# New issue orders for VectorE and ScalarE at the entries of a Strassen-Winograd convolution and of two feed-forward blocks

## The chip, the cores and the metric

The kernel runs on 1 core of one Trainium2 chip. The metric is device microseconds of one execution. Five engines work side by side, each through its own instructions in order: TensorE (PE, matmul; its weight loads are PEld), VectorE (DVE), ScalarE (ACT), GpSimd (POOL) and SyncE (SP); ACT, POOL and SP also issue DMA transfers. Engines wait for one another through semaphores only.

## The reference

A decoder trunk on x of 1024 tokens by 1024 features, all in fp32, two layers deep. With h = rms_norm(x, g) = x * rsqrt(mean(x*x) + 1e-6) * g:

```python
# layer 0                                   # layer 1
b, c, u = split(h @ w_in, 3)                q, k, v = h @ w_qkv        # 16 heads of 64
y = causal_depthwise_conv(c * u, 3 taps)    o = three dilated windows, merged by softmax of their lse
x = x + (b * y) @ w_out                     x = x + o @ w_out
# after each layer, a feed-forward block
x = x + (silu(h @ w_gate) * (h @ w_up)) @ w_down      # 1024 -> 2816 -> 1024
# at the end: rms_norm(x, final gain)
```

## The kernel before, in words

**Number format.** Every fp32 operand of a matmul is split into a high and a low part in a reduced format: ScalarE copies the high part (`split`, L139; `hi`, L567), VectorE subtracts it from the source for the low part (L140, L568). A product of blocks is three matmuls: high times high, high times low, low times high (L575, L576, L577 in `mm`). So twelve matmuls make one 128 x 512 output over a depth of 512: four operand tiles k = 0 to 3, three matmuls each; the low part of operand tile k is first read by the second of its three, the low part of the weight by the third matmul of the product.

**Winograd's form.** The convolution's input projection and both feed-forward blocks multiply 2 x 2 blocks with seven products instead of eight. The seven are numbered m = 1, 2, 6, 5, 7, 3, 4. The activations give seven operands (`b[m]`, four tiles each); the weights of one unit u (two output tiles of 128) give seven weight blocks, some of them sums of raw weight blocks made on VectorE (`combo`, L191). One product is (u, m). A unit's results gather in three PSUM banks: p takes m = 1, 6, 7, 4; q takes m = 2; r takes m = 5, 3. On the way ScalarE copies p out after m = 1, 6 and 7 (`save`, L581; tiles u1, u2, u3, each half a page of SBUF), and VectorE adds banks to them (`add`, L585): u1 + q is the output quarter (0, 0), made by `first`; u3 + r is quarter (1, 1), after m = 5 and 7; u2 + r is quarter (0, 1), after m = 3; p after m = 4 is quarter (1, 0). PSUM has eight banks, and a product that starts a bank waits until the earlier owner of that bank has been read; a product that adds to r waits until VectorE has read r.

**Orders.** `unit_order` writes the sequence of products by hand. At the start, unit by unit results are interleaved, since operands m = 6, 7, 5, 4, 3 are only made while m = 1 and 2 run. The product with index n in that order:
- convolution: (0,1) (1,1) (0,2) (1,2) (2,1) (2,2) (3,1) (3,2) (4,1) (4,2) (0,6) (1,6) (0,7) (1,7) (0,5) (1,5) (0,4) (1,4) (0,3) (1,3) (2,6) (2,5) (2,7) (3,6) ...
- first feed-forward block (key 0): (0,1) (1,1) (0,2) (1,2) (2,1) (2,2) (3,1) (3,2) (0,6) (1,6) (0,7) (1,7) (0,4) (1,4) (0,5) (1,5) (0,3) (1,3) (2,6) (2,5) (2,7) (3,6) ...
- second feed-forward block (key 1): (0,1) (1,1) (2,1) (3,1) (0,2) (1,2) (2,2) (3,2) (4,1) (4,2) (0,6) (1,6) (0,7) (1,7) (0,4) (1,4) (0,5) (1,5) (0,3) (1,3) (2,6) (2,5) (2,7) (3,6) ...

There is no planner: every engine's instructions are in the order in which the program issues them. After each product `products` calls `filled(n)`, and that calls `start(n)`, where the entry's further work is placed by n: next steps of the generator that makes operands (`operands` in the convolution, `second_half` in the feed-forward blocks), squares and sums for the norm, and `ensure(i)`, which issues weight sums and splits up to place i in the list of weights. `mm` itself calls `ensure` for `self.ahead` products ahead. `ensure` also makes SyncE fetch raw weight rows (512 KB each) into pages; a fetch waits for a free page. `at(u, m)` is the place of a weight in the list.

**The norm.** `stats` has two steps. The first sums the accumulated squares on TensorE (L485), takes the root on ScalarE (L488), the reciprocal (L489) and a diagonal matrix (L494) on VectorE; the second spreads the result over partitions by a matmul (L501) that ScalarE copies out (`rstd`, L502). Square root and Silu stand in different activation tables of ScalarE, so a root after other work begins with a table load; a dummy activation on a `scratch` column can make that load early. `flush` issues a sum of squares that was put off.

**The feed-forward entries.** The operands are made from scaled columns. `first_half` makes operands 1 and 2 from the left half of the columns while the layer before still writes the right half. `gained` scales the right half by the gain, and POOL adds two of these tiles by an accumulating DMA (L1183; `xd`). `second_half` scales them by `rstd` (L1187) and makes operands 7, 6, 4, 5, 3 in that order. `out` applies Silu to a gate quarter (L1239, ScalarE, even units) and multiplies the matching up quarter by it (L1242, VectorE, odd units); `store` sends quarters to DRAM on POOL's queue.

**Pages.** SBUF tiles of 128 x 1024 share 41 pages, half tiles 20 half pages; in the second block's entry x, operands, weight splits and raw rows fill the pages.

Of the kernel before, what the change touches and what calls it, by code (L numbers as in the profile page):

```python
# [95 lines left out]
def trunk(ctx: ExitStack, tc: tile.TileContext, x, gains_in, cwi, ck, cwo, wqkv, wo, relb,  # L96
# [444 lines left out]
    class Strassen:  # L541
# [75 lines left out]
        def whole(self, u, m, d):  # L617

            if m == 1:
                d["p"] = self.bank()  # L620
            elif m in (2, 5):
                d["q" if m == 2 else "r"] = self.bank()
            self.mm((u,), m, d["q" if m == 2 else "r" if m in (5, 3) else "p"], m in (1, 2, 5))
            if m in (1, 6, 7):
                d[{1: "u1", 6: "u2", 7: "u3"}[m]] = self.save(d["p"])
            if (u, m) == (0, 6):
                self.first(0)
            if m == 4:
                self.out(u, (1, 0), d.pop("p"))
            elif m == 3:  # L630
                self.out(u, (0, 1), self.add(d.pop("u2"), d.pop("r")))
            elif m in (5, 7) and "u3" in d and "r" in d:
                self.out(u, (1, 1), self.add(d.pop("u3"), d["r"]))
            early = self.key != 0
            if m == 2 and u > 3 + early or (u, m) in ((1, 3) if self.key == 1 else (0, 4), (3, 7)):
                for x in {u * (u < 2): range(4), 3: (4,) * early}.get(u, (u,)):
                    self.out(x, (0, 0), self.first(x))
                    del self.st[x]["u1"]

# [263 lines left out]
    class Conv(Strassen):  # L903
# [167 lines left out]
        def mix(self, group1):  # L1071
# [3 lines left out]
            def start(n):  # L1075
# [38 lines left out]
                elif n == 14:  # L1114
                    ensure(self.at(0, 3))
                    next(prep, None)
                    later = sums_of.pop(("m", (CONV, 2), 6))
                    ensure(self.at(1, 3))
                    later()
                    X[:] = [None] * KT  # L1120
                elif n == 18:
                    self.ahead = 3
                elif n == 19:
                    self.first(4)
                if 8 < n < 13:
                    self.squares((n - 5,), 1)
                if n == 16:
                    norm.joined()

            def gather():  # L1130
# [15 lines left out]
    class Swiglu(Strassen):  # L1146
# [27 lines left out]
        def gained(self, n):  # L1174
# [6 lines left out]
            if n > 3:  # L1181
                self.xd[n - 4] = self.xg[n - 4]
                nc.gpsimd.dma_start(out=self.xd[n - 4], in_=t, accum_op=ALU.add)  # L1183

        def second_half(self):

# [8 lines left out]
            if self.key:  # L1195
                yield
                self.first(0)
                self.first(1)
            for k in range(4):
# [14 lines left out]
            lows = [self.hi(4, k, f[4 + k]) for k in range(4)]  # L1214
            if self.key:
                for lo in lows:
                    lo()
                lows = []
            for k in range(4):
# [27 lines left out]
        def feed_forward(self, stats, last_step, after, final=None):  # L1247
            prep = []

            def start(n):  # L1250
# [6 lines left out]
                if n == 1 + self.key:  # L1257
                    next(stats)
                if n == 1:
                    if self.key:  # L1260
                        for m in (6, 7):
                            combos[self.key, 1](m)
                    ensure(self.at(0, 6))
                if n == 2 + 2 * self.key:
                    run(stats)
                    prep.append(self.second_half())
                    next(prep[0])
                    nc.scalar.activation(scratch, eps, AF.Silu)
                if n == 2:
                    ensure(self.at(1, 6))  # L1270
                elif n == 4:
                    ensure(self.at(1, 7))
                if n in ((5, 7, 8, 9, 11), (5, 6, 11, 12, 13, 16))[self.key]:
                    ensure(self.base + n + 3)
                    next(prep[0], None)

            self.run(start)
# [29 lines left out]
    def into_ffn(i, norm):  # L1307
# [50 lines left out]

        def last_step():
            run(pre[0])  # L1360
            norm.flush()

# [631 lines left out]
```

## Time and profile before

| | us |
|---|---|
| median of 3 runs (2137.76 to 2138.27) | 2137.87 |
| the profiled execution | 2138.59 |
| its span in the profile | 2136.8 |
| TensorE busy, share of the span | 2117.3, 99% |
| VectorE busy | 1718.8, 80% |
| ScalarE busy | 992.4, 46% |
| granted TensorE clock, mean | 0.998 |

The profiled execution's own time is 1.8 us more than its span. In the span, the convolution's first product starts at 5.5 us, the first feed-forward block's at 331.0 and the second one's at 1484.7; attention lies between. A line of a timeline reads: start, length, engine, line, operation, output<-inputs, shapes, count, and in brackets the idle time of the engine before it and what ended that. A line of the windows reads: stretch, then busy time and instruction count of PE, PEld, DVE, ACT and POOL, then the granted clock, the DMA share and GB/s.

### The profile page before, as it was taken

The numbers are of one execution on the slowest core, as the hardware profiler recorded it, in microseconds if no ns is written. First come the engines' busy times: TensorE is split into PE (matmuls) and PEld (weight loads), VectorE is DVE, ScalarE is ACT, GpSimd is POOL, SyncE is SP. The second block draws the span as 40 slices with busy tenths as digits, with TensorE's granted clock in tenths as the row PEclk, the third lists the DMA queues.
The fourth block names the chain that finished last, engine by engine and source line by source line (L and its number), as shares of the span: only waits on it lengthen the run. The fifth ranks groups of instructions, "written<-read, shape, count | busy, mean of one in ns | idle before, by whom it ended". The sixth has DMA issues, their size and how long they took to land.

```text
span 2136.8 us, 30748 instructions
## 1 busy us (share of the span) xinstructions
PE 2117.3 (99%) x11086; PEld 1815.5 (85%) x11086; DVE 1718.8 (80%) x3160; ACT 992.4 (46%) x1782; POOL 221.9 (10%) x316
## 2 busy tenths in 40 slices
PE   9999999999999999999999999999999999999998
PEld 7788888888888888878999999888788888888887
DVE  8898769888888888864676767768888888878876
ACT  7433336444544443344545454536544544444435
POOL 2000001111212000010111111110011212100000
PEclk9999999999999999999999999999999999999999
DMA  7222643334545784342333333635125545586432
GB/s 214 69 94 69 237 143 88 124 123 161 180 153 170 262 305 152 108 135 65 88 102 97 103 98 95 205 123 188 33 81 174 168 153 180 172 338 199 156 94 80
DMA packets 149347, 308.82 MB, mean 145 GB/s; under 512 B 50106, under 2 KB 61386, under 8 KB 149194
## 3 DMA queue, kind: packets, MB, share of 16 engines
q1 hardware_dynamic: 83306, 208.92, 30.6%
q0 software_dynamic: 25872, 79.02, 10.5%
q10 hardware_dynamic: 40016, 18.90, 3.0%
q8 instruction: 88, 1.44, 0.3%
q14 instruction: 65, 0.53, 0.1%
HBM read 209.06 MB, written 88.28 MB: 139 GB/s over the span
## 4 chain that ended last, share of the span: by engine, by line
PE 77%; issue 10%; DVE 7%; DMA 3%; ACT 2%; POOL 0%; SPq 0%; DVEq 0%; ACTq 0%; POOLq 0%
PE bank L575 16%; PE bank L577 16%; PE bank L576 16%; PE bank L1584 4%; PE bank L371 4%; PE bank L369 4%; PE bank L370 4%; PE bank L670 2%; PE bank L673 2%; PE bank L672 2%; PE bank L1444 1%; PE bank L1443 1%; PE bank L1442 1%; PE bank L1509 1%; PE bank L1508 1%
## 5 line engine op out<-in xcount | busy, mean ns | idle before, releaser
L575 PE MATMUL bank<-b,w 128*128 128x512 f32 x1816 | 710.0, 391 | 3.8 <-ACT w L139 2.2
L577 PE MATMUL bank<-b,w 128*128 128x512 f32 x1816 | 707.0, 389 | 2.1 <-DVE w L140 2.1
L576 PE MATMUL bank<-b,w 128*128 128x512 f32 x1816 | 707.7, 390 | 0.6 <-DVE b L568 0.3
L575 PEld LDWEIGHTS bank<-b,w 128*128 128x128 f32 x1816 | 341.1, 188 | 77.4 <-ACT w L139 5.2
L577 PEld LDWEIGHTS bank<-b,w 128*128 128x128 f32 x1816 | 341.0, 188 | 74.6 <-DVE w L140 3.4
L576 PEld LDWEIGHTS bank<-b,w 128*128 128x128 f32 x1816 | 341.2, 188 | 71.2 <-DVE b L916 1.1
L139 ACT ACTIVATE w<-combo 128x512 fp32r<-128x512 f32 (+2 forms) x448 | 229.3, 540 | 249.6 <-DVE combo L191 229.7
L140 DVE TENSOR_TENSOR w<-combo,w 128x512 fp32r<-128x512 f32 (+2 forms) x448 | 254.7, 581 | 30.8 <-ACT w L139 30.5
L581 ACT ACTIVATE part<-bank 128x512 f32<-128x512 f32 x168 | 100.2, 597 | 295.9 <-PE bank L577 292.2
L140 DVE TENSOR_TENSOR w<-raw,w 128x512 fp32r<-128x512 f32 (+2 forms) x308 | 169.4, 568 | 23.3 <-ACT w L139 23.1
L585 DVE TENSOR_TENSOR part<-part,bank 128x256 f32<-128x256 f32 (+1 forms) x328 | 154.2, 500 | 35.4 <-ACT part L581 20.0
L139 ACT ACTIVATE w<-raw 128x512 fp32r<-128x512 f32 (+2 forms) x308 | 150.9, 527 | 63.8 <-DMA raw<-in_ffn_w_down 19.1
L831 DVE TENSOR_TENSOR x<-x,bank 128x512 f32<-128x512 f32 x168 | 114.7, 683 | 37.2 <-PE bank L577 34.6
L369 PE MATMUL bank<-w_hi,w 128*128 128x512 f32 (+1 forms) x320 | 119.6, 374 | 0.0
L371 PE MATMUL bank<-w_hi,w 128*128 128x512 f32 (+1 forms) x320 | 117.8, 368 | 0.3 <-DVE w L140 0.3
L370 PE MATMUL bank<-w_lo,w 128*128 128x512 f32 (+1 forms) x320 | 117.7, 368 | 0.0
L506 DVE TENSOR_TENSOR x<-x,bank 128x512 f32<-128x512 f32 (+1 forms) x104 | 66.0, 642 | 56.0 <-PE bank L371 47.0
L369 PE MATMUL bank<-h_hi,w_hi 128*128 128x512 f32 x256 | 104.4, 408 | 0.0
L191 DVE TENSOR_TENSOR combo<-raw 128x512 f32<-128x512 f32 (+1 forms) x160 | 103.2, 645 | 0.0
L371 PE MATMUL bank<-h_hi,w_lo 128*128 128x512 f32 x256 | 100.0, 391 | 0.2 <-DVE w_lo L140 0.2
L370 PE MATMUL bank<-h_lo,w_hi 128*128 128x512 f32 x256 | 99.9, 390 | 0.0
L1603 ACT ACTIVATE z<-bank 64x512 f32<-64x512 f32 x32 | 19.0, 594 | 160.6 <-PE bank L1584 160.4
(266 smaller groups left out, 3816.7 us busy)
## 6 DMA issues: line engine op xcount, KB each, us to landing
hin<-part SPq DMA_DIRECT2D x126, 256.0 KB
raw<-in_ffn_w_gate SPq DMA_DIRECT2D x44, 512.0 KB
raw<-in_ffn_w_up SPq DMA_DIRECT2D x44, 512.0 KB
b<-ready SPq DMA_DIRECT2D x42, 512.0 KB
part<-sum POOLq DMA_DIRECT2D x72, 256.0 KB, 3.5
raw<-in_ffn_w_down SPq DMA_DIRECT2D x48, 384.0 KB
x<-spill SPq DMA_DIRECT2D x24, 512.0 KB
raw<-in_attn_w_qkv SPq DMA_DIRECT2D x24, 512.0 KB
```

What stands on the lines that cost most here:

```text
L139: nc.scalar.activation(hi, src, AF.Copy)
L140: eng.tensor_tensor(out=lo, in0=src, in1=hi, op=ALU.subtract)
L191: eng.tensor_tensor(out=c, in0=a, in1=b, op=op)
L369: nc.tensor.matmul(b, whi[:, a], ahi[:, s], start=first, stop=False)
L370: nc.tensor.matmul(b, whi[:, a], alo[:, s], start=False, stop=False)
L371: nc.tensor.matmul(b, wlo[:, a], ahi[:, s], start=False, stop=last)
L575: nc.tensor.matmul(b, hi[:, a], bhi, start=start and k == 0, stop=False, skip_group_check=True)
L576: nc.tensor.matmul(b, hi[:, a], blo, start=False, stop=False, skip_group_check=True)
L577: nc.tensor.matmul(b, lo[:, a], bhi, start=False, stop=k == n - 1, skip_group_check=True)
L581: nc.scalar.activation(t, b, AF.Copy)
L585: nc.vector.tensor_tensor(out=t, in0=t, in1=b, op=ALU.add)
L831: nc.vector.tensor_tensor(out=X[n][:, half(h)], in0=X[n][:, half(h)], in1=b, op=ALU.add)
```

## The change

Five groups of edits; no arithmetic is added or taken away, except one dummy root on one column.

- Quarters: in the feed-forward blocks quarter (0, 0) of units 0 to 3 was put out together, after (0,4) in the first block and after (1,3) in the second. Now units 0 and 1 are put out after (0,4), units 2 and 3 after (2,5), in both. The convolution's order of quarters stays.
- Convolution: clearing X, the weight split of (1,3) and the weight sums of unit 2 go from n = 14 to n = 15; the join of the two sums of squares from n = 16 to n = 18, followed by a dummy root; splits run three products ahead from n = 20 instead of 18.
- Second block, start: the copies of p after m = 1 of units 0 to 2, the weight sums of unit 1 and the splits (now up to (4,2)) are issued at n = 2, behind the root and its diagonal; the spread of `rstd` and the first part of `second_half` at n = 3 instead of 4. The splits of m = 6 follow at n = 5, those of m = 7 at n = 6.
- Second block, operands: `second_later` takes the rest in other portions, at n = 4, 5, 6, 7, 11, 13, 15, 16.
- Both blocks: `last_step` flushes the last sum of squares ahead of the last low part of operand 2.

```diff
@@ Strassen.whole
-            if m in (1, 6, 7):
+            if m in (6, 7) or m == 1 and not (self.key == 1 and u < 3):
                 d[{1: "u1", 6: "u2", 7: "u3"}[m]] = self.save(d["p"])
...
             early = self.key != 0
-            if m == 2 and u > 3 + early or (u, m) in ((1, 3) if self.key == 1 else (0, 4), (3, 7)):
-                for x in {u * (u < 2): range(4), 3: (4,) * early}.get(u, (u,)):
-                    self.out(x, (0, 0), self.first(x))
-                    del self.st[x]["u1"]
+            done = {(0, 4): range(4), (3, 7): (4,) * early}
+            if self.key != CONV:
+                done.update({(0, 4): (0, 1), (2, 5): (2, 3)})
+            for x in (u,) if m == 2 and u > 3 + early else done.get((u, m), ()):
+                self.out(x, (0, 0), self.first(x))
+                del self.st[x]["u1"]
@@ Conv.mix, start
                 elif n == 14:
                     ensure(self.at(0, 3))
                     next(prep, None)
+                elif n == 15:
                     later = sums_of.pop(("m", (CONV, 2), 6))
                     ensure(self.at(1, 3))
                     later()
                     X[:] = [None] * KT
-                elif n == 18:
+                elif n == 20:
                     self.ahead = 3
...
-                if n == 16:
+                if n == 18:
                     norm.joined()
+                    nc.scalar.activation(scratch, eps, AF.Sqrt)
@@ Swiglu, new
+        def second_later(self, low7, t3, t2, h, f, rstd, tt):
+
+            def operand(m, x):
+                for lo in [self.hi(m, k, x[k]) for k in range(4)]:
+                    lo()
+
+            self.first(0)
+            for k in range(4):
+                tt(t2[k], t3[k], f[k], ALU.add)
+            yield
+            self.first(1)
+            for lo in low7:
+                lo()
+            yield
+            operand(6, t2)
+            for k in range(4):
+                tt(f[4 + k], f[4 + k], t2[k], ALU.subtract)
+            for k in range(4):
+                tt(h[k], h[k], rstd, ALU.mult)
+            yield
+            for k in range(4):
+                tt(f[k], h[k], t2[k], ALU.subtract)
+            yield
+            operand(4, {k: f[4 + k] for k in range(4)})
+            yield
+            operand(5, f)
+            yield
+            lows = [self.hi(3, k, h[k]) for k in range(4)]
+            for lo in lows[:2]:
+                lo()
+            yield
+            for lo in lows[2:]:
+                lo()
+            X[:] = [None] * KT
@@ Swiglu.second_half
             if self.key:
                 yield
-                self.first(0)
-                self.first(1)
+                yield from self.second_later(low7, t3, t2, h, f, rstd, tt)
+                return
...
             lows = [self.hi(4, k, f[4 + k]) for k in range(4)]
-            if self.key:
-                for lo in lows:
-                    lo()
-                lows = []
@@ Swiglu.feed_forward, start
                 if n == 1 + self.key:
                     next(stats)
-                if n == 1:
+                if n == 1 + self.key:
                     if self.key:
+                        for u in range(3):
+                            self.st[u]["u1"] = self.save(self.st[u]["p"])
                         for m in (6, 7):
                             combos[self.key, 1](m)
-                    ensure(self.at(0, 6))
-                if n == 2 + 2 * self.key:
+                        ensure(self.at(4, 2))
+                    else:
+                        ensure(self.at(0, 6))
+                if n == 2 + self.key:
                     run(stats)
                     prep.append(self.second_half())
                     next(prep[0])
                     nc.scalar.activation(scratch, eps, AF.Silu)
-                if n == 2:
+                if n == 2 and not self.key:
                     ensure(self.at(1, 6))
-                elif n == 4:
+                elif n == 4 and not self.key:
                     ensure(self.at(1, 7))
-                if n in ((5, 7, 8, 9, 11), (5, 6, 11, 12, 13, 16))[self.key]:
+                if n in ((5, 7, 8, 9, 11), (4, 5, 6, 7, 11, 13, 15, 16))[self.key]:
                     ensure(self.base + n + 3)
                     next(prep[0], None)
+                if self.key and n in (5, 6):
+                    ensure(self.at(1, n + 1))
@@ into_ffn, last_step
+            norm.flush()
             run(pre[0])
-            norm.flush()
```

## The prediction

> **What bounds the kernel now.** I read the page's part 1, then the TensorE waits, then the TensorE timeline around each wait, then VectorE's and ScalarE's timelines there.
>
> ```profile
> PE 2117.3 (99%) x11086; PEld 1815.5 (85%) x11086; DVE 1718.8 (80%) x3160; ACT 992.4 (46%) x1782; POOL 221.9 (10%) x316
> ...
> 60.00:65.00 5.00, 3.44 (x16) 2.81 (x16) 4.96 (x9) 1.62 (x3) 0.00 (x0) 1.00 0.30 100
> ...
> 1595.00:1600.00 5.00, 5.00 (x24) 4.14 (x23) 2.93 (x6) 2.63 (x5) 0.00 (x0) 1.00 0.01 2
> ```
>
> TensorE sets the end; whatever is to be won is the time in which its next matmul starts late. A matmul's row lasts 0.39 but the next starts 0.23 later, and a product of twelve takes 2.72:
>
> ```profile
> 1506.76 0.39 PE L575 MATMUL bank<-b,w 128*128 128x512 f32 x1
> ...
> 1509.48 0.40 PE L575 MATMUL bank<-b,w 128*128 128x512 f32 x1
> ```
>
> So lateness is read from starts. Here are the late starts at the three entries, each with its predecessor where one is needed (convolution; first FFN; second FFN):
>
> ```profile
> 59.70 0.39 PE L577 MATMUL bank<-b,w 128*128 128x512 f32 x1
> 61.65 0.47 PE L575 MATMUL bank<-b,w 128*128 128x512 f32 x1 [1.56 <-ACT w L139]
> ...
> 336.26 0.39 PE L577 MATMUL bank<-b,w 128*128 128x512 f32 x1
> 337.09 1.05 PE L485 MATMUL bank<-ones,acc 128*128 128x1 f32 x8 [0.44 <-DVE acc L470]
> ...
> 374.65 0.40 PE L576 MATMUL bank<-b,w 128*128 128x512 f32 x1
> 375.73 0.50 PE L577 MATMUL bank<-b,w 128*128 128x512 f32 x1 [0.68 <-DVE w L140]
> ...
> 1499.08 0.39 PE L577 MATMUL bank<-b,w 128*128 128x512 f32 x1
> 1500.31 1.12 PE L501 MATMUL bank<-diag,ones 128*128 128x512 f32 x2 [0.84 <-DVE diag L494]
> 1501.51 0.40 PE L576 MATMUL bank<-b,w 128*128 128x512 f32 x1
> ...
> 1531.03 0.39 PE L577 MATMUL bank<-b,w 128*128 128x512 f32 x1
> 1531.58 0.50 PE L575 MATMUL bank<-b,w 128*128 128x512 f32 x1 [0.15 <-ACT gate L1239]
> ...
> 1535.28 0.47 PE L575 MATMUL bank<-b,w 128*128 128x512 f32 x1 [0.69 <-DVE gate L1242]
> ...
> 1538.69 0.49 PE L575 MATMUL bank<-b,w 128*128 128x512 f32 x1 [0.41 <-ACT b L567]
> 1539.51 0.50 PE L576 MATMUL bank<-b,w 128*128 128x512 f32 x1 [0.33 <-DVE b L568]
> ...
> 1550.55 0.39 PE L576 MATMUL bank<-b,w 128*128 128x512 f32 x1
> 1552.20 0.50 PE L577 MATMUL bank<-b,w 128*128 128x512 f32 x1 [1.27 <-DVE w L140]
> ```
>
> Convolution: 61.65-59.70-0.23 = 1.72. First FFN: 337.09-336.26-0.23 = 0.60 and 375.73-374.65-0.23 = 0.85, together 1.45. Second FFN: 1500.31-1499.08-0.23 = 1.00; 1531.58-1531.03-0.23 = 0.32; then, by whole products, 1535.28-1531.58-2.72 = 0.98 and 1538.69-1535.28-2.72 = 0.69; 1539.51-1538.69-0.23 = 0.59; 1552.20-1550.55-0.23 = 1.42; together 5.00. The sum is 8.17 us: nearly all that this change can win.
>
> A rule bears on how to count this. The idle times in the brackets add to 6.37 us only. The Trainium skill (Perfetto Trace Analysis, Identifying the Most-Contended Engine) calls matmul busy time a bad measure, because matmuls are pipelined, and sends the reader to weight-load time. The row of 60 to 65 agrees: weight loads fall from 4.14 to 2.81, which is 1.6 us of a slice, nearer to 1.72 than to the 1.56 idle. By idle time the forecast below would be 1.8 us later; I go by the starts.
>
> **Convolution.** The profile names ScalarE's split as what ended the 1.56, but that split is the weight of (2,6), one product later. Product (1,3), which starts at 61.65, adds into the bank that VectorE reads for (1,5):
>
> ```profile
> 58.90 0.68 DVE L140 TENSOR_TENSOR w<-combo,w 128x512 fp32r<-128x512 f32 x1
> ...
> 60.82 0.68 DVE L585 TENSOR_TENSOR part<-part,bank 128x512 f32<-128x512 f32 x1
> 61.42 1.22 DVE L449 TENSOR_TENSOR acc<-acc,acc 128x1024 f32<-128x1024 f32 x1
> ...
> 61.00 1.15 ACT L139 ACTIVATE w<-combo 128x512 fp32r<-128x512 f32 x2 [3.37 <-DVE combo L191]
> ```
>
> The read ends at 61.50; the product starts 0.15 later. The change issues the weight low (58.90), the two combinations between, and the clearing of X one product later, so the read takes the place of the low at 58.90 and ends at 59.58 (VectorE runs without a pause here). (1,3) can start at 59.93 (59.70+0.23): 1.72 gone. What is late next: the low of (1,3) now ends at 60.18, needed 0.45 into the product (60.38); the combinations end at 61.51, ScalarE's high of (2,6) at 62.2, its low at 62.9; (2,6) starts at 62.65 and needs the low at 63.10. Both margins are about 0.2, so up to 0.3 may come back. The join of the squares (1.22) moves behind that low and ends near 64.7; the sums read it after (2,6), at 65.4. The weight splits made two instead of three products ahead for two products, and the rows that SyncE fetches for them, come 2.72 later but are first needed at (2,5) and (2,7), 2 us after they are made. The early root adds one instruction to ScalarE; its table load moves. Prices from the second FFN's pair of the same kind:
>
> ```profile
> 1505.27 1.28 ACT L1268 ACT_TABLE_LOAD   x1
> 1506.57 0.20 ACT L1268 ACTIVATE scratch<-eps 128x1 f32<-128x1 f32 x1
> ```
>
> 1.5 us on ScalarE after 62.2 lie in its idle time (3.37 before 61.00); the next high, of (2,5), is then ready at 64.4 for a product at 67. Convolution: -1.7 (0 to +0.3 back).
>
> **First FFN.** The flush ahead of the last low swaps two VectorE rows:
>
> ```profile
> 335.74 0.69 DVE L568 TENSOR_TENSOR b<-hcol,b 128x512 fp32r<-128x512 f32 x1 [0.16 <-ACT b L567]
> 336.35 0.69 DVE L470 TENSOR_TENSOR acc<-acc,sq 128x512 f32<-128x512 f32 x1
> ...
> 372.40 1.28 DVE L585 TENSOR_TENSOR part<-part,bank 128x512 f32<-128x512 f32 x2
> 373.78 0.69 DVE L1242 TENSOR_TENSOR part<-part 128x512 f32<-128x512 f32 x1
> ...
> 374.99 0.68 DVE L140 TENSOR_TENSOR w<-combo,w 128x512 fp32r<-128x512 f32 x1
> ```
>
> The add then ends at 336.18, before the product ahead ends (336.49): 0.60 gone. The low ends at 336.8, for a product that starts at 337.4. Quarters: units 2 and 3 leave (0,4) for (2,5), so the 2 adds, 1 multiply, 1 Silu and 1 store on POOL's queue are issued seven products later. The low of (1,5) at 374.99 moves ahead by 3 x 0.6 = 1.8, more than the 0.85 it is late. Two banks and two half pages are held longer; with p0, p1, q0 and q1 free by then, the next banks find room. What bounds this unseen hold: 0, or a bank wait as in the rows of 1531.58 and 1535.28 (0.32 to 0.98); I take 0, because four banks are free. First FFN: -1.45.
>
> In the second FFN the flush changes nothing (its add is issued earlier already).
>
> **Second FFN.** VectorE's 128x512 rows start 0.60 apart (four in 2.50), ScalarE's 0.52 (four in 2.19):
>
> ```profile
> 1494.30 1.06 ACT L581 ACTIVATE part<-bank 128x512 f32<-128x512 f32 x2
> 1495.25 2.19 ACT L139 ACTIVATE w<-raw 128x512 fp32r<-128x512 f32 x4
> ...
> 1498.33 0.27 ACT L488 ACTIVATE r<-bank,eps 128x4 f32<-128x4 f32 x1
> ...
> 1502.10 2.50 DVE L1187 TENSOR_TENSOR x<-x,rstd 128x512 f32<-128x512 f32 x4 [1.25 <-ACT rstd L502]
> 1507.32 1.29 DVE L140 TENSOR_TENSOR w<-combo,w 128x512 fp32r<-128x512 f32 x2 [2.73 <-ACT w L139]
> ...
> 1530.94 0.58 ACT L1239 ACTIVATE gate<-bank 128x512 f32<-128x512 f32 x1
> ```
>
> and the accumulating transfers, by their line:
>
> ```profile
> L1183 POOL DMA_DIRECT2D x<-x x4: 842/850/882, 1487.8 to 1494.7; - x4
> ...
> DMA to landing us min/median/max: 6.9/7.6/8.5
> ```
>
> Root: at 1498.33 it stood behind saves and splits; now it is ahead of them, at 1494.30. Reciprocal and diagonal (0.9) end near 1495.5, and the spread is read after (3,1), which ends at 1499.31-2.72 = 1496.59. The 1.00 goes; the spread's own 0.97 (1501.51-1500.31-0.23) stays.
>
> Scalings: ScalarE does three saves (1.5), four splits (2.2), one save and the spread (1.1) and is at 1499.3; VectorE does three combinations and four lows and is at 1499.9. The first scaling starts there, 2.2 earlier. The fourth needs the last accumulating transfer, which lands near 1501.6 (last issue 1494.7, and 6.9), so the scalings end at 1502.4. Then twelve VectorE rows (two quarters, four sums, four lows, two weight lows; 7.2) and four lows: operand 6 is complete at 1512.0. (0,6) starts at 1496.59+0.97+6x2.72 = 1513.9: margin 1.9, paid out of VectorE's idle 1.25 and 2.73.
>
> Banks: with p of five units and q of units 2, 3 and 4 all eight are taken, so (0,5) waits for ScalarE's gate (1530.94, queued behind operand 5's highs) and (1,5) for VectorE's gate. With the work ahead done, (1,7) ends at 1513.9+4x2.72 = 1524.8; ScalarE then does one save, one split and four highs (3.3), and reads the gate by 1528.7, before (0,5) at 1530.2. VectorE's gate ends at 1532.0, before (1,5) at 1533.0. 0.32 and 0.98 go.
>
> Operand 3 is split one product earlier but two of its lows are queued behind an add, two combinations and a weight low: from 1524.8 I count 4.5 to the first quarter's multiply (those 3.3 and two Silus), twelve rows of 0.6 and the low's own 0.7, so the third low ends 12.4 after and is wanted 4x2.72+7x0.23 = 12.5 after, and (1,3) finds its bank read at 13.6, just when it is due. So nothing is left over, and I keep 0.3 of the 0.69+0.59 = 1.28. Bounds: 0 to one product, 2.72. I take 0.3, since each count comes from rows of this stage. The 1.42 goes, because the low of (2,7) is issued before the quarters that now come at (2,5). Second FFN: -5.00+0.3 = -4.7.
>
> **Sum.** 1.7+1.45+4.7 = 7.85. A start after a wait is followed by a step of 0.31 to 0.34 instead of 0.23 (61.65, 1531.58), 0.1 at each of five waits: 8.3. The profiled execution took 2138.59 (span 2136.8 and 1.8 around it): 2130.3. It lies 0.7 above the median 2137.87, so the median to expect is 2129.6.
>
> **Rivals.** (B) The second FFN re-forms one wait: VectorE runs a product later than I count and TensorE is held once for up to 2.72, most likely at operand 3's late lows. For it: margins of 0.1. Against: 1.9 at (0,6). 2129.6+2.72 = 2132.3.
> (C) VectorE is the bound: its rows are full (4.96 of 5 at 60 to 65), no VectorE work is taken away, and the waits reappear one product on; only root and flush stay won (1.6) and about 1 of the rest. 2135.3. Against: the idle 1.25 and 2.73 just ahead.
> (D) Slower: scalings wait for the accumulating transfers. The six weight rows of 512 KB fetched for (4,1) and (4,2) are now issued a product later, beside them. Each us of landing beyond 1501.6+1.9 delays (0,6) by one; it decides beyond 1503.5+8.3 = 1511.8, and a landing at 1514 gives 2140. Against: landings took 8.5 at most. The Trainium skill (Trainium Kernel Development and Optimization, Key Constraints) has all issuing queues share the same 16 DMA engines; the long landings agree.
>
> **How the numbers follow.** Forecast 0.62, B 0.18, C 0.14, D 0.06. This kernel's measurement tells 0.2%, 4.3 us, from no change: faster is forecast and B, 0.80; same C; slower D. The forecast alone spans 2128.2 (every wait and 1.4 of start-up steps gone) to 2131.5. The range is carried to 2134.0, over B and the near edge of C.
>
> **What would show it.** Right: no TensorE wait at (1,3) of the convolution, at the sums of the first FFN and at the spread of the second; the root there before 1495; the first scaling near 1500; gates read before (0,5). Wrong: TensorE waits of over 1 us between (0,6) and (2,7), or a scaling ended by a transfer's landing after 1504.

## The result and the profile after

The changed kernel takes 2128.27 us (median of 4 runs, 2127.97 to 2128.81) against 2138.07 for the kernel before (4 runs, 2137.76 to 2138.28): a ratio of 0.9954, with a 95% interval of 0.9942 to 0.9966. That is 9.8 us less. The forecast was 2129.6 in a range of 2128.2 to 2134.0. The profiled execution took 2128.81, with a span of 2127.0.

To see where the time went, the starts of the same matmul in two traces are compared. Every kernel here issues the same 11,086 matmuls in the same order, except that the two matmuls of the second block's spread come one product earlier where that block has its new order (one product later in a_spread_later). So the difference of start times between two quiet places, where no matmul is late, tells what the stage between them has gained. Between before and after, the convolution's entry gains 1.74, the first feed-forward entry 1.83 and the second one 5.14 (1.15 up to product (1,4), 3.99 from (0,5) on): 8.71 together. Another 1.1 of the 9.8 of the spans lies outside these stages; the last two runs deal with that.

**Convolution.** The slice of 60 to 65 us after, in the view of equal stretches (columns: TensorE, weight loads, VectorE, ScalarE, GpSimd, then clock, DMA share, GB/s):

```profile
60.00:65.00 5.00, 5.00 (x23) 4.05 (x22) 4.21 (x7) 2.64 (x4) 0.00 (x0) 1.00 0.45 145
```

TensorE holds 23 matmuls where it held 16, and VectorE is no longer full (4.21 of 5). The timelines of TensorE and VectorE there show why:

```profile
60.41 0.39 PE L577 MATMUL bank<-b,w 128*128 128x512 f32 x1
60.64 0.39 PE L575 MATMUL bank<-b,w 128*128 128x512 f32 x1
...
59.60 0.68 DVE L585 TENSOR_TENSOR part<-part,bank 128x512 f32<-128x512 f32 x1
60.20 0.68 DVE L140 TENSOR_TENSOR w<-combo,w 128x512 fp32r<-128x512 f32 x1
...
62.97 0.69 DVE L140 TENSOR_TENSOR w<-combo,w 128x512 fp32r<-128x512 f32 x1 [0.76 <-ACT w L139]
...
64.17 1.22 DVE L449 TENSOR_TENSOR acc<-acc,acc 128x1024 f32<-128x1024 f32 x1
```

The bank of (1,5) is read at 59.60, ahead of the low, and (1,3) starts at 60.64, one ordinary step (0.23) after the matmul ahead of it. The split that the profile of before named as the releaser of this product comes at 62.30 now, 1.7 after the product has started: it never was what (1,3) waited for. The low of (2,6) ends at 63.66; (2,6) starts at 63.41 and needs it 0.45 later, at 63.86. So the forecast margin of 0.2 is there.

**First feed-forward.** The same two timelines after:

```profile
335.27 0.39 PE L577 MATMUL bank<-b,w 128*128 128x512 f32 x1
335.49 0.95 PE L485 MATMUL bank<-ones,acc 128*128 128x1 f32 x8
...
373.03 0.39 PE L576 MATMUL bank<-b,w 128*128 128x512 f32 x1
373.26 0.39 PE L577 MATMUL bank<-b,w 128*128 128x512 f32 x1
...
334.50 0.69 DVE L470 TENSOR_TENSOR acc<-acc,sq 128x512 f32<-128x512 f32 x1
```

The put-off sum of squares ends at 335.19, and the sums start on time. The third matmul of (1,5), late by 0.85 before, follows in 0.23.

**Second feed-forward.** This stage begins 3.06 earlier than before (1481.66 against 1484.72), so 3.06 has to be added to compare with the prediction's times. TensorE, ScalarE and VectorE after:

```profile
1493.28 0.40 PE L577 MATMUL bank<-b,w 128*128 128x512 f32 x1
1493.52 1.02 PE L501 MATMUL bank<-diag,ones 128*128 128x512 f32 x2
...
1510.72 0.39 PE L575 MATMUL bank<-b,w 128*128 128x512 f32 x1
...
1527.04 0.39 PE L575 MATMUL bank<-b,w 128*128 128x512 f32 x1
...
1529.76 0.39 PE L575 MATMUL bank<-b,w 128*128 128x512 f32 x1
...
1491.23 0.24 ACT L488 ACTIVATE r<-bank,eps 128x4 f32<-128x4 f32 x1
...
1524.90 0.59 ACT L1274 ACTIVATE gate<-bank 128x512 f32<-128x512 f32 x1
...
1496.66 2.49 DVE L1226 TENSOR_TENSOR x<-x,rstd 128x512 f32<-128x512 f32 x4
...
1506.29 2.49 DVE L568 TENSOR_TENSOR b<-x,b 128x512 fp32r<-128x512 f32 x4
...
1527.85 0.68 DVE L1277 TENSOR_TENSOR gate<-bank,gate 128x512 f32<-128x512 f32 x1
```

Root 1494.29 (forecast 1494.30), spread 1496.58 (1496.59), first scaling 1499.72 (1499.9), operand 6 complete at 1508.78+3.06 = 1511.84 (1512.0), (0,6) at 1513.78 (1513.9) with a margin of 1.94 (1.9); ScalarE's read of the gate ends 1.55 before (0,5) starts, VectorE's 1.23 before (1,5). The view of TensorE's waits between 1484 and 1560 has no entry any more. What is left is at operand 3:

```profile
1533.84 0.39 PE L575 MATMUL bank<-b,w 128*128 128x512 f32 x1
1534.12 0.50 PE L576 MATMUL bank<-b,w 128*128 128x512 f32 x1
1534.46 0.39 PE L577 MATMUL bank<-b,w 128*128 128x512 f32 x1
...
1533.38 1.28 DVE L568 TENSOR_TENSOR b<-x,b 128x512 fp32r<-128x512 f32 x2
```

The third low of operand 3 ends at 1534.06, the matmul that reads it starts at 1534.12 (a step of 0.28), the next step is 0.34, and (1,3) begins with one of 0.31: 0.25 over the ordinary steps, where 0.3 was kept.

### The profile page after: what moved, and what is told of

It reads as the page before. It is cut to its first block, busy times and chain, and to the rows that moved or that the text cites. A ratio compares the mean times of both kernels' runs of the same rounds, so it can differ in the third digit from the quotient of the medians.

```text
span 2127.0 us, 30749 instructions
## 1 busy us (share of the span) xinstructions
PE 2115.9 (99%) x11086; PEld 1816.2 (85%) x11086; DVE 1718.5 (81%) x3160; ACT 991.6 (47%) x1783; POOL 221.8 (10%) x316
## 4 chain that ended last, share of the span: by engine, by line
PE 95%; DVE 2%; DMA 1%; ACT 1%; issue 1%; SPq 0%; ACTq 0%; DVEq 0%
PE bank L576 19%; PE bank L575 19%; PE bank L577 19%; PE bank L371 6%; PE bank L369 6%; PE bank L370 6%; PE bank L1625 4%; PE bank L672 2%; PE bank L675 2%; PE bank L674 2%; PE bank L1485 1%; PE bank L1484 1%; PE bank L1483 1%; PE bank L1550 1%; PE bank L1549 1%; DMA x<-spill 1%
```

## The experiments

Each kernel ran beside the kernel before on the same chip. The table gathers all of them; the stage columns are differences of matmul starts against the first profile of before, "outside" is what the span gained beyond the three entries, "tail" is the part of it that lies after the last matmul's start, and the last column is the median against the median of before taken beside it.

| kernel | convolution | first FFN | second to (1,4) | second from (0,5) | sum | outside | tail | median |
|---|---|---|---|---|---|---|---|---|
| after | -1.74 | -1.83 | -1.15 | -3.99 | -8.71 | -1.08 | -1.32 | -9.80 |
| p_conv | -1.79 | -0.01 | -0.05 | -0.01 | -1.86 | -2.60 | -1.21 | -2.80 |
| p_flush_quarters | -0.04 | -1.83 | +0.01 | -0.95 | -2.81 | -2.29 | -1.24 | -3.74 |
| p_second | -0.03 | +0.02 | -1.17 | -2.94 | -4.12 | +0.22 | -1.60 | -4.95 |
| b_banks | +0.02 | +0.02 | -0.01 | -1.40 | -1.37 | -0.17 | -0.89 | -0.76 |
| a_no_root | -1.75 | -1.79 | -1.17 | -3.97 | -8.68 | -1.47 | -0.82 | -8.91 |
| a_join_early | -1.51 | -1.79 | -1.17 | -3.96 | -8.43 | -1.54 | -1.20 | -9.12 |
| a_read_late | -0.03 | -1.84 | -1.15 | -3.99 | -7.01 | -2.95 | -1.26 | -8.85 |
| a_spread_later | -1.79 | -1.82 | +0.64 | -3.96 | -6.93 | -2.75 | -0.86 | -8.12 |
| a_acc_late | -1.77 | -1.79 | -1.17 | -3.98 | -8.71 | -1.43 | -0.83 | -8.96 |
| a_three_lows | -1.74 | -1.79 | -1.15 | -3.99 | -8.67 | -0.45 | -1.21 | -8.16 |
| a_again | -1.77 | -1.81 | -1.17 | -4.01 | -8.76 | -1.49 | -1.21 | -9.53 |
| b_again | +0.01 | -0.04 | -0.04 | +0.04 | -0.03 | +0.41 | -0.04 | +0.36 |

Where an entry was not edited, its column repeats within 0.06. The medians scatter by about 1 us, their intervals are wider still, so verdicts below go by the stages.

### One part of the change at a time

**p_conv**: the kernel before with the convolution's edits alone.

```diff
+                elif n == 15:
                     later = sums_of.pop(("m", (CONV, 2), 6))
                     ensure(self.at(1, 3))
                     later()
...
-                if n == 16:
+                if n == 18:
                     norm.joined()
+                    nc.scalar.activation(scratch, eps, AF.Sqrt)
```

> The kernel before with the convolution's part of the change alone. Theory (TensorE's late start at product (1,3) comes from VectorE's read of the bank of (1,5), which the joined multiply and its wait for the root stood ahead of): the start of the product after the entry moves by -1.7, both feed-forward entries keep their waits, total -1.7 (2136.3). Rival 1 (the wait is the split that the profile names): (1,3) still starts 1.7 late, total 0. Rival 2 (VectorE is the bound): no wait at (1,3), but one of 1 to 1.7 at a later product of the entry, total 0 to -0.7. The 0.33 and 0.40 found at the first down-products should not be here.

2134.86 us; ratio 0.9987 (0.9978 to 0.9996). The entry gains 1.79 and (1,3) starts without a wait. Both rivals fall: the wait neither stays nor comes back later in the entry.

**p_flush_quarters**: the flush ahead of the last low, and the quarters of units 2 and 3 at (2,5).

```diff
+            done = {(0, 4): range(4), (3, 7): (4,) * early}
+            if self.key != CONV:
+                done.update({(0, 4): (0, 1), (2, 5): (2, 3)})
...
+            norm.flush()
             run(pre[0])
-            norm.flush()
```

> The kernel before with the swap of the flush and units 2 and 3's quarters moved from (0,4) to (2,5) in both feed-forwards alone; the second one keeps its early order. Theory (each wait is its own): first FFN -0.5 at the sums and -1.3 at the low of (1,5); second FFN -1.4 at the low of (2,7), its spread, bank and operand-3 waits stay (1.00+0.32+0.98+1.28): total -3.2 to -3.9 (2134.2 to 2134.9), the upper end if the 0.33 and 0.40 found at the first down-products belong to the quarters. Rival (VectorE is the bound, C): in the second FFN the 1.42 comes back as a wait of 1 to 1.5 at (1,3) or (2,5), total -1.8 to -2.2.

2133.92 us; ratio 0.9983 (0.9974 to 0.9992). The first feed-forward gains all that it gains in the full change, 1.83. The second gains 0.95, not 1.4, so the stages give 2.81 together, less than the 3.2 to 3.9 expected. The wait at the low of (2,7) is gone there (1.52 with the slow step that follows it), and the rival's wait of 1 to 1.5 at (1,3) or (2,5) does not come; but 0.57 comes back at the two bank waits ahead of them. In the timelines of TensorE and VectorE of this kernel:

```profile
1533.40 0.47 PE L575 MATMUL bank<-b,w 128*128 128x512 f32 x1 [0.99 <-DVE gate L1244]
...
1530.77 0.68 DVE L1244 TENSOR_TENSOR part<-part 128x512 f32<-128x512 f32 x1
...
1532.58 0.68 DVE L1244 TENSOR_TENSOR gate<-bank,gate 128x512 f32<-128x512 f32 x1
```

In the kernel before, the second block's quarters came at (1,3). This edit brings those of units 0 and 1 to (0,4), and with that one multiply (1530.77) ahead of the gate's multiply that frees the bank for (1,5): that wait grows from 0.98 to 1.30 (1533.40-1529.38-2.72). The rest, 0.27 at (0,5), goes with ScalarE's gate, which stands behind a high that started 0.3 later after its operand was ready than in the kernel before; what held it I could not see. In the full change the same multiply stands ahead of the gate (1526.03), and the gates have 1.2 to 1.6 in hand, so it costs nothing.

**p_second**: the second feed-forward's new order alone, with its quarters where they were, at (1,3) (the expectation says (0,4), which is where the first block has them).

```diff
-            if m in (1, 6, 7):
+            if m in (6, 7) or m == 1 and not (self.key == 1 and u < 3):
...
+                yield from self.second_later(low7, t3, t2, h, f, rstd, tt)
+                return
...
-                if n == 2 + 2 * self.key:
+                if n == 2 + self.key:
                     run(stats)
```

> The kernel before with the rearranged start of the second feed-forward alone (saves, root and spread a product earlier, adds and lows in the new portions); its quarters stay at (0,4), the convolution and the first FFN as before. Theory (each wait is its own): -1.0 at the spread, -1.3 at the two bank waits, about -1.1 at operand 3, the wait of 1.42 at the low of (2,7) stays: total -3.4 to -3.8 (2134.1 to 2134.5). Rival (the two halves need each other, VectorE's backlog only moves): the spread's 1.0 goes and the rest reappears between (0,4) and (2,7) as one wait of 2.5 to 3.5, total -1.0 to -1.5.

2132.71 us; ratio 0.9979 (0.9970 to 0.9988). The stage gains 4.11: spread, bank and operand 3's waits are gone, and what is left is the wait at the low of (2,7), in TensorE's timeline:

```profile
1548.42 0.39 PE L576 MATMUL bank<-b,w 128*128 128x512 f32 x1
1549.84 0.50 PE L577 MATMUL bank<-b,w 128*128 128x512 f32 x1 [1.03 <-DVE w L140]
```

It is 1549.84-1548.42-0.23 = 1.19, a little less than the 1.42 of before. The rival, one wait of 2.5 to 3.5 in the same stretch, falls. The three parts give 1.79+1.83+0.95+4.11 = 8.68 in their stages, the full change 8.71: the gains add in sum. They do not add wait by wait: the 0.57 that the quarters alone give back at the banks is not there in the full change, and the rest of 0.25 at operand 3 in the full change is not there in p_second. That the two sums meet so closely is in part chance.

### Is VectorE full?

**b_banks**: the kernel before, with two of VectorE's bank reads issued earlier in the second block.

```diff
+                if n == 10 and self.key:
+                    self.first(2)
+                    self.first(3)
```

> The kernel before with two of VectorE's bank reads (units 2 and 3, two instructions of 0.6 each) moved ahead, so that two more banks are free before (0,5) and (1,5) of the second feed-forward. Theory (the waits of 0.32 and 0.98 at (0,5) and (1,5) are for banks): both go, but since 1.2 of VectorE's work now stands ahead of operand 3's lows, (0,3) starts later by about as much as is won; total 0 to -0.5. Rival 1 (the two bank waits are worth their time by themselves): -1.3 (2136.7). Rival 2 (VectorE's work ahead of the lows decides alone): slower by 1.2 (2139.3).

2136.90 us; ratio 0.9994 (0.9985 to 1.0003). The stage gains 1.40. The timed gain, 0.76, is not clear of noise; the reading rests on the stage. The waits at (0,5) and (1,5) go, so they were for banks. The one at (0,3) grows from 0.69 to 1.73, and up to there nothing is won. That size was expected, but not for the reason given. TensorE's and ScalarE's timelines of this kernel at operand 3:

```profile
1539.85 0.49 PE L575 MATMUL bank<-b,w 128*128 128x512 f32 x1 [1.52 <-ACT b L567]
...
1539.18 2.18 ACT L567 ACTIVATE b<-x 128x512 fp32r<-128x512 f32 x4
```

ScalarE's first high of operand 3 starts at 1538.02 in the kernel before and 1.16 later here, as the whole stage does (1.19): the two reads push nothing back. TensorE now comes 1.1 earlier to an operand that is ready no sooner. But the low of (2,7) is in time, a term that my expectation had left out. VectorE's timeline of before and then of this kernel:

```profile
1521.79 0.69 DVE L140 TENSOR_TENSOR w<-raw,w 128x512 fp32r<-128x512 f32 x1 [1.22 <-ACT w L139]
```

```profile
1521.69 1.28 DVE L585 TENSOR_TENSOR part<-part,bank 128x512 f32<-128x512 f32 x2
1522.97 0.69 DVE L140 TENSOR_TENSOR w<-raw,w 128x512 fp32r<-128x512 f32 x1
```

The two reads (1.28) fill 1.22 us in which VectorE had waited for ScalarE, and the batch of quarters ahead of the low of (2,7) is shorter by them. No work was taken away, and the stage is 1.40 shorter. So VectorE's volume of work was not the bound here (rival C); the order of its queue was.

### What made (1,3) of the convolution late

**a_read_late**: the changed kernel with the bank's read behind the low and the two combinations again, the join left late.

```diff
-                elif n == 15:
                     later = sums_of.pop(("m", (CONV, 2), 6))
```

> The changed kernel with one edit of the convolution undone: the low of product (1,3)'s weight and the two combinations of (2,6) are issued ahead of VectorE's read of the bank of (1,5) again, as before; the join's multiply stays at its new, later place. Theory (this bank read alone made (1,3) late; the join back at its old place cost only 0.3): the read starts 1.9 later, (1,3) starts 1.0 to 1.7 late, total +1.0 to +1.7 (2129.3 to 2130.0). Rival (read and join were both needed, or the join was the cause): less than 0.3 late. Rival of the profile's named releaser (the split of (2,6)): 0.

**a_join_early**: the changed kernel with the join put back, the read left early.

```diff
-                if n == 18:
+                if n == 16:
                     norm.joined()
+                if n == 18:
                     nc.scalar.activation(scratch, eps, AF.Sqrt)
```

> The changed kernel with the join's multiply of the convolution's entry put back two products, to where it stood before; the bank's read stays ahead of it only by the rest of the new order. Theory (what made (1,3) wait was VectorE held in the join ahead of the bank's read): the join is a multiply that VectorE waits in until ScalarE's sums are there, so part of the 1.75 comes back, between 0.2 (only the low of (2,6) late) and 1.7 (the bank's read behind it again): 2128.5 to 2130.0. Rival (the releaser that the profile names, the split, was the cause): 0.

With the read late, 2129.06 us, the entry loses all it had gained (-0.03). In TensorE's and VectorE's timelines:

```profile
59.36 0.39 PE L577 MATMUL bank<-b,w 128*128 128x512 f32 x1
61.29 0.47 PE L575 MATMUL bank<-b,w 128*128 128x512 f32 x1 [1.54 <-ACT w L139]
...
60.46 0.68 DVE L585 TENSOR_TENSOR part<-part,bank 128x512 f32<-128x512 f32 x1
```

(1,3) starts 0.15 after the read's end (61.14), as before, and the profile again names ScalarE's split, which is not the cause. With the join early, 2128.49 us, the entry loses 0.23: (1,3) is in time, and the join's 1.22 stand ahead of the low of (2,6):

```profile
63.11 0.39 PE L576 MATMUL bank<-b,w 128*128 128x512 f32 x1
63.52 0.50 PE L577 MATMUL bank<-b,w 128*128 128x512 f32 x1
...
61.64 1.22 DVE L449 TENSOR_TENSOR acc<-acc,acc 128x1024 f32<-128x1024 f32 x1
62.78 0.69 DVE L140 TENSOR_TENSOR w<-combo,w 128x512 fp32r<-128x512 f32 x1
```

So the read is worth 1.7, and moving the join keeps the 0.2 that the reordering would else give back at the next product.

**a_no_root**: the changed kernel without the early root on scratch (no output depends on it).

```diff
                     norm.joined()
-                    nc.scalar.activation(scratch, eps, AF.Sqrt)
```

> The changed kernel without the root written to scratch near the end of the convolution's entry (its result is read by nobody; it only has the table of the roots loaded before the real root of the join). Theory (the load of 1.28 lies in ScalarE's idle time either way, and what follows waits for VectorE): 0 (2128.3), the load then stands at the real root near 68. Rival (the load would stand on the way to the next operand): +1.3 (2129.6).

2128.70 us, the entry at -1.75 as with it. ScalarE's timeline of this kernel:

```profile
66.46 1.28 ACT L488 ACT_TABLE_LOAD   x1
67.76 0.27 ACT L488 ACTIVATE r<-bank,eps 128x8 f32<-128x8 f32 x1
```

The load moves to the real root. By the clock of the changed kernel (this trace is 0.76 ahead) that root starts 0.47 later, and the split behind it is on time. This line of the change is worth nothing here.

### How much slack the second block has

**a_spread_later**: the changed kernel with roots, spread, first adds and scalings of the second block put off.

```diff
-                if n == 2 + self.key:
+                if n == 2 + 3 * self.key:
                     run(stats)
...
-                if n in (..., (4, 5, 6, 7, 11, 13, 15, 16))[self.key]:
+                if n in (..., (6, 7, 8, 9, 11, 13, 15, 16))[self.key]:
...
-                if self.key and n in (5, 6):
-                    ensure(self.at(1, n + 1))
+                if self.key and n in (7, 8):
+                    ensure(self.at(1, n - 1))
```

> The changed kernel with the second feed-forward's reciprocal roots, their spread and the first adds and scalings put off by two to three products (about 3.7 to 4 us later on VectorE). Theory (the margin at (0,6) is 1.9, so the first 1.9 are free and the rest shows): (0,6) starts 1.8 to 2.2 late, total +1.8 to +2.5 (2130.1 to 2130.8). Rival C (VectorE has no slack, all of it shows): +3.7 to +4 (2132). Rival (the weights, not the scalings, set (0,6)): 0.

2129.49 us; the stage loses 1.79 up to (1,4), for scalings that are 4.0 late (this stage starts 1.78 earlier than in the profile of after, so 1498.87 compares with 1496.66-1.78 = 1494.88). TensorE and VectorE:

```profile
1514.83 0.39 PE L576 MATMUL bank<-b,w 128*128 128x512 f32 x1
1516.47 0.50 PE L577 MATMUL bank<-b,w 128*128 128x512 f32 x1 [1.26 <-DVE w L140]
...
1498.87 2.50 DVE L1226 TENSOR_TENSOR x<-x,rstd 128x512 f32<-128x512 f32 x4 [3.88 <-ACT rstd L502]
...
1515.73 1.29 DVE L140 TENSOR_TENSOR w<-combo,w 128x512 fp32r<-128x512 f32 x2
```

The size is the expected one, the place is not: (0,6) still starts on time, 0.2 is lost inside it, and 1.5 at (0,7), whose weight's low (1515.73) is issued behind eight VectorE rows for later operands.

**a_acc_late**: rival D made to happen: the last accumulating transfer issued after ScalarE's saves and splits.

```diff
             next(pre[0], None)
-            sw.gained(k)
+            if not i or k < 7:
+                sw.gained(k)
...
+                    if self.key:
+                        self.gained(7)
                     run(stats)
```

> The changed kernel with the last of the four accumulating transfers of the second feed-forward (and the scaling on ScalarE that feeds it) issued after the saves and splits instead of ahead of the root, some 4.8 later. This is the prediction's rival D made to happen. Theory: it is issued near 1496.4 and lands near 1503, VectorE's fourth scaling waits for it and is 4.5 late; since a shift of 4.0 of all scalings showed 1.7, the slack is 2.3: TensorE late by 2 to 2.5 at (0,6) or (0,7), total +2 to +2.5 (2130.3 to 2130.8). Rival (slack is larger for one late scaling, the others go ahead): 0 to +0.5. By the prediction's own words (each us of landing beyond 1503.5 delays (0,6) by one; shifted by the 3.1 won ahead, beyond 1500.4): +2.6.

2128.95 us, and no stage loses anything; the theory's 2 to 2.5 misses, and the rival of a larger slack comes out. The issue of the last transfer on GpSimd's queue and the scaling that waits for it, in this kernel:

```profile
1495.35 0.84 POOL L1187 DMA_DIRECT2D x<-x  x1 [4.81 <-ACT x L1183]
...
1498.55 0.69 DVE L1226 TENSOR_TENSOR x<-x,rstd 128x512 f32<-128x512 f32 x1 [0.81 <-DMA x<-x]
```

It is issued 3.7 later than in the changed kernel (1491.61); this trace is 0.64 ahead there, so within its stage it is 4.4 later. It is there after 3.2 us. In the changed kernel the four take 7.4 in the median, in the view of the transfers between 1484 and 1500:

```profile
x<-x POOLq DMA_DIRECT2D x4, 256.0 KB, 7.4
```

VectorE waits 0.81, inside its slack. By the clock of before (this stage starts 3.70 earlier) the landing is at 1502.2 at the latest, ahead of the 1503.5 from which the prediction had it cost anything: what missed is the landing that I expected; what the prediction says of a landing beyond that was not reached. While this late transfer runs, all transfers together move 36 to 210 GB/s, against 220 to 348 in the 4 us after its issue in the changed kernel (the views of the transfers between 1484 and 1500, by slices of 0.4 us): it meets fewer others. Whether it lands sooner for want of weight fetches, or of its own predecessors in GpSimd's queue, was not told apart. The Trainium skill (Trainium Kernel Development and Optimization, Key Constraints) has the queues of all issuing engines share 16 DMA engines; these two durations agree with it but do not test it.

**a_three_lows**: three of operand 3's lows a portion earlier.

```diff
-            for lo in lows[:2]:
+            for lo in lows[:3]:
                 lo()
             yield
-            for lo in lows[2:]:
+            for lo in lows[3:]:
```

> The changed kernel with three instead of two of operand 3's lows issued in the portion before the last. Theory (the rest of 0.25 at the third low of (0,3), three late steps of 0.28 to 0.34 near 1534 to 1536, is this low standing behind a quarter's add and two combinations): -0.25 (2128.0), no late step there. Rival (the row that then comes later, the read of a bank for (1,3), takes its place): 0 to +0.3.

2129.45 us, the stage at -3.99 as without it. The third low's wait goes, and the bank read that it was moved past takes its place (with one more slow step, 0.32, behind the matmul that reads the fourth low), in TensorE's and VectorE's timelines:

```profile
1535.96 0.48 PE L575 MATMUL bank<-b,w 128*128 128x512 f32 x1
...
1535.13 0.68 DVE L585 TENSOR_TENSOR part<-part,bank 128x512 f32<-128x512 f32 x1
```

Here the rival holds: the read ends at 1535.81 and (1,3) starts 0.15 later. At this place VectorE's queue is full, and for the last 0.25 rival C is right.

### The time outside the stages

**a_again** and **b_again**: the changed kernel and the kernel before, each unaltered.

> The changed kernel unaltered, timed again. The stages of the change give -1.75 (convolution), -1.82 (first FFN) and -5.16 (second FFN), -8.7 in all; the three parts by themselves gave -1.81, -1.91 and -0.98, -4.12 in their stages, -8.8. Theory (the first times' -9.8 holds 1.1 that lies outside these stages, in the landings of first loads, of the down-projection's weights and the tail, which differ from one execution to the next): -8.5 to -9.5. Rival (the change wins beyond its stages): -9.8 again, with the first down-products' steps of 326 and 349 ns and a tail of 3.4 in the new profile too.

> The kernel before unaltered, with a profile of its own. In the profiles of twelve variants the stages outside the three entries are shorter than in the first profile of before by 0.2 to 3.0 (median 1.4; the tail after the last matmul alone by 0.8 to 1.6), also where only one entry differs. Theory (the first profile of before was a long one there; start, weight landings and tail differ from one execution to the next): stages of the entries 0.0 within 0.1, the rest shorter by 0.5 to 2, tail near 7.0 instead of 8.2, time as before within 0.1%. Rival (any of the changes shortens the tail and the down-projections too): the rest within 0.3 of the first profile, tail 8.2 again.

The changed kernel took 2128.38 us, a ratio of 0.9956 (0.9944 to 0.9969), 9.5 less than the 2137.91 beside it. The kernel before took 2138.41 against 2138.05 (ratio 1.0, 0.9991 to 1.0009). Its second profile bears out one half of the theory and one half of the rival. The wait at the first down-products of the two blocks (0.43 and 0.53 in the first profile of before) is 0.65 and none in the second, and runs from none to 0.9 in kernels with the same work there: it differs between executions. But the tail, here the whole time from the last matmul's start to the end of the span, is 8.2 us in both profiles of before and 6.6 to 7.4 in all twelve others. The view of the transfers over the last 9 us (40 slices, busy tenths of the DMA engines, then packets, MB and share of the queue that loads instructions), first of the kernel before, then after:

```profile
DMA  0000000599999999999999917995111000000000
...
q14 instruction: 2, 0.02, 0.9%
```

```profile
DMA  0000000000003999999999999999999300000000
...
q14 instruction: 2, 0.02, 0.5%
```

In the kernel before, the output's transfers nearly stop for one slice (0.2 us), and the last ones trail on few engines. In its second profile they fall to half for two slices instead, and trail too. The instructions' two packets take 0.9% in both profiles of before, but 0.8% also in p_flush_quarters and a_acc_late, whose tails are 7.0 and 7.4; so they are not shown to be the reason. With any of the edits, even b_banks with two instructions moved, the tail is shorter. So about 1.2 us of the 9.8 are won at the outputs, where nothing that was edited runs. Why the kernel before has the longer tail in both its profiles, and no variant has it, stays open.

None of the variants beats the changed kernel.

## Why the prediction was right, and where it was off

- **The late starts as the sum to win** (8.17, less 0.3 kept): 8.71 was won with 0.25 left over, where idle time gave 6.37. One argument for starts was misread: weight loads that fall from 4.14 to 2.81 are 1.61 us of a slice, nearer to the 1.56 idle than to 1.72. The 0.16 between the two is the 0.39 of a row less the 0.23 of a step, and the 1.74 that the entry gained decides for the starts. The waits named are the ones that went; none of more than 0.3 came back between (0,6) and (2,7), and the marks set (root before 1495, first scaling near 1500, gates read before (0,5)) hold.
- **Convolution, -1.7**: 1.74 measured. That the profile's releaser was not the cause is shown by a_read_late, and the next margin, 0.2, by a_join_early. The early root was priced as costing nothing; it also brings nothing.
- **First FFN, -1.45**: 1.83 measured. The term that was mis-sized is the low of (1,5). By whole products, before:

```profile
374.34 0.48 PE L575 MATMUL bank<-b,w 128*128 128x512 f32 x1
...
378.22 0.47 PE L575 MATMUL bank<-b,w 128*128 128x512 f32 x1
```

  378.22-374.34-2.72 = 1.16, not 0.85: the steps around the late one are slow too (0.31 at 374.65, 0.34 at 376.07, 0.32 at 378.22). I added 0.1 for each of five waits, 0.5; going by stages, 8.71-(8.17-0.25) = 0.8 belongs there.
- **Second FFN, -4.7**: 5.14 measured, for the same reason: slow steps after the waits and at the spread. Within it the order of events came out within 0.2 us of each forecast time. That the quarters' part is worth 1.42 by itself was too simple: alone it gives back 0.57 at the banks, and only the early order hides that.
- **Rival B** (one wait re-forms) and **rival C** (VectorE is the bound): the changed kernel's waits view, b_banks and p_second speak against them, except for the last 0.25 at operand 3.
- **Rival D**: it took the landing time of a transfer as 6.9 to 8.5 and let it grow with the fetches beside it; a_acc_late shows 3.2 for one issued later, so even a much later issue stays inside the slack. What a landing beyond 1503.5 would cost was not tried.
- **The time**: 8.7 in the stages and 1.2 at the outputs are 9.9, where 9.8 and 9.5 were measured. So close an agreement is in part chance: in b_banks the same sum, 1.40 and 0.89, is 1.5 more than its medians show. The forecast of 2129.6 was 1.3 high: 0.4 from the slow steps after waits, and most of the rest from the tail, which it did not have. By the stages alone it would have come out at about 2129. The measured 2128.27 lies 0.07 above the lower end of the range. That end was argued from every wait gone and 1.4 of start-up steps, which came to 0.8; the gain at the outputs, which was not forecast, made up the difference, so that the time came out so near the edge and still inside it is luck.

## What to carry to other kernels

Read lost time from the start of each matmul against the ordinary step, by whole products, and include the slow steps after a wait; the idle time in the brackets and the releaser that it names can both mislead when several semaphores are waited for. When an engine's queue seems full, look for the waits inside it: moving a short instruction into one can free a later one by its whole length. The gains of moves at different waits added in sum here, but test the parts together too: one part alone gave back 0.57 that the other part hides. Compare stages, not only totals: stages that were not edited repeated within 0.06 us where medians of whole runs differed by 1.

## What was not expected of the hardware

- A 256 KB accumulating transfer took 3.2 us when issued 4.4 us later (a_acc_late), against a median of 7.4 amid the weights' fetches (6.6 to 8.3 in the changed kernel).
- After a wait on VectorE or ScalarE, TensorE's next step takes 0.31 to 0.34 us instead of 0.23 (0.31 after 61.65, 0.34 after 1531.58, 1539.51 and 1552.20 in the kernel before), so a wait costs about 0.1 more than its late start shows; with slow steps before and behind it, as at (1,5) of the first block, 0.3 more.
- A table load on ScalarE takes 1.28 us; at both places where the convolution's load was put (62.95 and 66.46) the activation after it starts 0.02 later.
- The kernel before ends 8.2 us after its last matmul's start in both of its profiles, with output transfers that slow down late and trail; twelve kernels with the same outputs, edited elsewhere, end after 6.6 to 7.4.
